# A hybrid decoder layer: one function table for Ln and Exp, a side projection in 16 products, another order list

## The chip, the cores and the metric

One Trainium2 chip, one core of it. The metric is the device time of one execution in microseconds (us), as the median of several runs. Five engines matter: PE (TensorE, matrix products), DVE (VectorE), ACT (ScalarE), POOL (GpSimd) and SP (SyncE, which issues most DMAs). Each engine works through its own queue in order.

## The reference

One decoder layer on x of 512 tokens by 1024 channels, in float32:

```python
x = x + 0.5 * swiglu(rms_norm(x, ffn1_norm), ...)            # d_ff = 2816
x = x + hybrid_mixer(rms_norm(x, mix_norm), ...)
x = x + 0.5 * swiglu(rms_norm(x, ffn2_norm), ...)
return rms_norm(x, final_norm)

def hybrid_mixer(h, ...):
    proj = h @ w_in                                          # one input projection
    gates = sigmoid(proj[..., aw + rs:] + gate_bias)
    y_attn = dilated_attention(proj[..., :aw], positions) @ attn_w_up
    y_rwkv = rwkv7_time_mix(token_shift(proj[..., aw:aw + rs], mu), ...)
    return (gates[..., :1024] * y_attn + gates[..., 1024:] * y_rwkv) @ w_o
```

`rwkv7_time_mix` has 16 heads of 64: a normalised key (`kk / sqrt(sum kk^2)`), a state recurrence over the tokens, a normalisation of its output per head (`(y - mean) / sqrt(var + eps)`), a bonus term and an output gate `sigmoid(zg) @ g2` with zg of 160 columns. `dilated_attention` has 3 groups of 4 heads, merged by their softmax denominators.

## The kernel before

Every large product is made of float32r products on PE. Weights and activations are split into a high and a low part (ACT copies the high part, DVE subtracts it), and a tile of 128 output channels by 512 tokens is the sum of 8 x 3 = 24 products of 128x128 by 128x512 (`mm3`: high x high, high x low, low x high). A weight tile of 512 KB comes by one DMA on SP's queue, three raw tiles ahead. The small products of the mixer are in plain float32.

The kernel has three parts: the first feed-forward, the mixer and the second feed-forward. In the mixer the main stream is a list of tiles, `MAIN`: two tiles of the small streams (`zwa`, `zg`), the 24 tiles of r, k and v (one of each per pair of heads), 16 gate tiles, 18 attention tiles (`aq`, `ak`, `av`, two halves by three groups), 8 tiles of `wout` (the recurrence's output projection, which needs all eight `yf`), two of `aup`, 8 of `wo`. Their order between `zwa`, `zg` and `wo` is written out by hand in `MAIN_ORDER`.

Between them runs side work, in three chains. `lora_all` and then `post(0)` to `post(7)` prepare one pair of heads each, from its k, r and v. `finish(0)` to `finish(3)` run the recurrence of two pairs each in 8 chunks one after another, and then `tail`, which normalises, gates and stores `yf`. `core(0)` and `core(1)` are the attention of one half each; `core` begins when its last key tile, `ak.<half>.2`, is there. A reciprocal square root (`rsqrt`) is an Ln and an Exp on ACT with one Newton step on DVE; `post` has one for the key and `tail` has one for the variance of each pair, 16 in all.

The mixer isn't issued as it is written. `Plan` records each instruction as a `Node` with a price (`note`), finds what depends on what, and simulates the five engines (`order`): it takes again and again the instruction that can start first, main products being placed between the side work. `emit` then issues the instructions in that order, which fixes every engine's queue. Prices are lines such as

```python
TABLES = {"Sigmoid": "sigmoid", "Tanh": "sigmoid", "Exp": "exp", "Ln": "exp", "Sqrt": "sqrt", "Silu": "silu"}
c = n / 2400 + 0.0136 if x.dtype == F32R else 4 * n / 2400 + 0.01      # us on PE; n is the free size
if nd.table and nd.table != table:                                     # ACT: another table
    c += 1.3
```

A plain float32 transpose of 128x128 is thus priced at 4 x 128 / 2400 + 0.01 = 0.223 us. The plan knows a switch of tables, and Ln and Exp are one table to it. The emitter issues no table load itself in the mixer; the tool chain places loads where an activation needs one.

`h_zg2` makes the last 32 columns of the gate stream: 24 products with 32 weight columns (`w_zg2`, split by `lora_w`), then `shift_evac` (token shift), a sigmoid and a split into `sg2`.

Of the kernel before, what the change touches and what calls it, by code (L numbers as in the profile page):

```python
# [45 lines left out]
WAHEAD = 2  # L46

MAIN_ORDER = """
k.0 r.0 v.0 k.1 r.1 v.1 gate.0 gate.1 gate.2 gate.3 k.2 gate.4 r.2 v.2 r.3 k.3 v.3 gate.5 gate.6 gate.7 gate.8 k.4 r.4
v.4 k.5 r.5 gate.9 v.5 gate.10 gate.11 gate.12 gate.13 gate.14 gate.15 k.6 r.6 v.6 k.7 r.7 v.7 aq.0.0 av.0.0 aq.0.1  # L50
ak.0.1 av.0.1 aq.0.2 ak.0.0 av.0.2 ak.0.2 av.1.2 av.1.0 aq.1.0 aq.1.1 ak.1.0 ak.1.1 av.1.1 aq.1.2 ak.1.2 wout.0 wout.1
wout.2 wout.3 wout.4 wout.5 wout.6 aup.0 wout.7 aup.1"""


PE, DVE, ACT, POOL, SP = "PE", "DVE", "ACT", "POOL", "SP"
LAT, SLACK, WINDOW, HOLD, SETTLE = 0.07, 0.2, 40, 0.0, 3.5
URGENT, SIDE, MAIN_MM = range(3)


class Node:  # L60
# [25 lines left out]
class Plan:  # L86


    TABLES = {"Sigmoid": "sigmoid", "Tanh": "sigmoid", "Exp": "exp", "Ln": "exp", "Sqrt": "sqrt", "Silu": "silu"}

    def __init__(self):
        self.on = False
# [38 lines left out]
    def note(self, eng, op, call, outs, ins, func=None):  # L131
        tags = [k[0] for k in map(self.slot, outs + ins) if k]
        if eng == PE:
            w, x = ins[0], ins[1]
            n, k, m = x.free_size(), w.shape[0], w.free_size()
            mode = (32 if k <= 32 else 64 if k <= 64 else 128, 32 if m <= 32 else 64 if m <= 64 else 128)
            c = n / 2400 + 0.0136 if x.dtype == F32R else 4 * n / 2400 + 0.01
            c = 0.018 if mode == (32, 32) else c * 0.5 if 64 in mode else c
            nd = self.open
            if nd is None:  # L140
                nd = self.open = Node(PE, self.cls, len(self.nodes))
                nd.mode = [mode, mode]
                self.placed(nd)
            elif nd.mode[1] != mode:
                c += 0.1
                nd.mode[1] = mode
            nd.cost += c
        else:
            self.open = None
            urgent = any(t.startswith(("wraw", "whi", "wlo")) for t in tags) or any(t.startswith("acc") for t in tags)  # L150
            nd = self.placed(Node(eng, URGENT if urgent else self.cls, len(self.nodes)))
            n = max([x.free_size() for x in outs + ins], default=0)
            psum = any(x.space == PSUM for x in outs + ins)
            if op == "dma_start":
                nd.cost = 0.43
                nd.lands = 4
                for c in outs[0].shape:
                    nd.lands *= c
            elif eng == ACT:
                nd.cost = 0.2 + n * 0.00084 if n else 1.3  # L160
                nd.table = self.TABLES.get(func)
            elif eng == POOL:
                nd.lock = op != "memset"
                nd.cost = 0.2 + n * (0.0022 if nd.lock else 0.00065)
            else:
                nd.lock = not psum
                nd.cost = 0.14 + n * {"reciprocal": 0.0063, "tensor_tensor_scan": 0.0028}.get(op, 0.00107)
        nd.calls.append(call)
        nd.writes += [(self.region(x), x.space == DRAM, self.slot(x)) for x in outs]
        nd.reads += [(self.region(x), x.space == DRAM, self.slot(x)) for x in ins]  # L170
# [46 lines left out]
    def order(self, keep):  # L217
# [19 lines left out]
        for nd in self.nodes:  # L237
            for tag in {k[0] for k in uses[nd]}:
                touch.setdefault(tag, []).append((nd, [k for k in nd.new if k[0] == tag], [k for k in uses[nd] if k[0] == tag and k in mortal]))

        def safe(nd):

            for tag in {k[0] for k in nd.new}:
                bufs = next(k[1] for k in nd.new if k[0] == tag)
                u = used.get(tag, 0) + sum(k[0] == tag for k in nd.new)
                if u > bufs:
                    return False
                rest = {}
                l = touch[tag] = [x for x in touch[tag] if x[0] not in done]
                for m, new, ends in l:  # L250
                    if m is not nd:
                        u += len(new)
                        if u > bufs:
                            return False
                    for k in ends:
                        n = rest[k] = rest.get(k, left[k]) - 1
                        if not n:
                            u -= 1
            return True

        while len(done) < len(self.nodes):
# [25 lines left out]
            if eng == SP or nd.lands:  # L287
                free[eng] = t + c
                dma = max(dma, t + c) + nd.lands / 190e3
                end = dma + 1.8  # L290
            elif eng == PE:
                if nd.mode[0] != mode:
                    c += 0.2 if nd.mode[0] == (128, 128) else 0.1
                mode = nd.mode[1]
                free[PE] = t + c
                end = t + c + 0.17
            else:
                if nd.table and nd.table != table:
                    c += 1.3
                    table = nd.table  # L300
                if nd.lock:
                    t = max(t, port)
                    port = t + c
                end = free[eng] = t + c
# [7 lines left out]
            for k in nd.new:  # L312
# [2 lines left out]
                freed[k[0]].remove(f)  # L315
                self.place[k[2]] = f[1]
            for k in uses[nd]:
                left[k] -= 1
                if not left[k] and k in mortal:
                    used[k[0]] -= 1  # L320
                    freed.setdefault(k[0], []).append((end, self.place.get(k[2])))
# [27 lines left out]
    def emit(self, tc, keep):  # L349
        self.on = False  # L350
        with tc.manual_schedule():
            for nd in self.order(keep):
                for tag, _, name in nd.new:
                    if tag in self.rings:
                        (pool, at), (shape, dt) = self.place[name], self.tiles[name]
                        self.homes[name] = pool.tile(list(shape), dt, tag=at, bufs=1, name=name)
                for f, args, kw in nd.calls:
                    f(*map(self.put, args), **{k: self.put(x) for k, x in kw.items()})  # L358
        self.nodes = []
# [332 lines left out]
def mixer(tc, a, env):  # L692
# [17 lines left out]
    with ExitStack() as st:  # L710
# [87 lines left out]
            split(z[:, 0:S], sg[:, 0, :], sg[:, 1, :])  # L798

        def h_zg2(ps):  # L800
            z = shift_evac(ps, 2, 32)
            A.activation(z[0:32, 0:S], z[0:32, 0:S], AF.Sigmoid)
            split(z[0:32, 0:S], sg2[0:32, :], sg2[32:64, :])
            A.copy(sg2[64:96, :], sg2[0:32, :].bitcast(F32))
# [318 lines left out]
        def tail(q, Qt, YT, raws):  # L1123
            for hl in range(2):
                hp = 2 * q + hl
                w = lora_w(raws[hl])
                A.copy(w[64:96, P:2 * P], w[64:96, 256 + P:512].bitcast(F32))
                sq = b2()
                A.activation(sq[:, 0:S], YT[:, hl, :], AF.Square)
                sh = split2(sq[:, 0:S])  # L1130
                ps = headsum(sh)
                rs = b2()
                V.tensor_scalar(rs[:, 0:S], ps, 1.0 / 64.0, GN_EPS, op0=ALU.mult, op1=ALU.add)
                rs = rsqrt(rs)
                V.scalar_tensor_tensor(rs[:, 0:S], YT[:, hl, :], col("ln_w", hp), rs[:, 0:S], op0=ALU.mult, op1=ALU.mult)
                bon = b2()
                Y.dma_start(bon[:, 0:S], bnd[:, hp, :])
                V.scalar_tensor_tensor(rs[:, 0:S], rs[:, 0:S], col("ln_b", hp), bon[:, 0:S], op0=ALU.add, op1=ALU.add)
                pg = mi()
                mm3(T, pg, (w[:, 0:P], w[:, 256:256 + P]), (sg[:, 0, :], sg[:, 1, :]), True, False)  # L1140
                T.matmul(pg, w[0:96, P:2 * P], sg2, start=False, stop=True)
                V.tensor_mul(rs[:, 0:S], rs[:, 0:S], pg)
                Y.dma_start(yf[:, hp, :], rs[:, 0:S])
# [123 lines left out]
        mrg = {}  # L1267
        ssq = acts.tile([P, S], F32, tag="ssqa", bufs=1, name="ssq_m")
        rstd = None
        wz = lora_w(lora_load(a["w_zg2"]))  # L1270
        for t in MAIN:
            n = t[0]
            w = wnext(t)
            if n in handlers:
# [8 lines left out]
                if n == "zg":  # L1283
                    ps = acc()
                    plan.stream = "main"
                    for k in range(DC):
                        plan.cls = MAIN_MM
                        mm3(T, ps[0:32, :], wsl((wz[:, 0:256], wz[:, 256:512]), k, 32), xk(k), k == 0, k == DC - 1)
                        plan.cls = SIDE
                        plan.cut()  # L1290
                    plan.stream = "main"
                    h_zg2(ps)
# [154 lines left out]
```

## Time and profile before

| | |
|---|---|
| time, median of 3 runs | 1404.8 us (1403.41 to 1405.29) |
| profiled execution, own time | 1407.91 us |
| its span, first to last instruction | 1406.1 us |
| PE, DVE, ACT, POOL busy | 97%, 59%, 43%, 1% of the span |
| granted PE clock, mean | 0.990 |
| mixer | some 365 to 1045 us of the span |

Products are pipelined, so that a busy PE isn't PE at its peak. "Idle before" an instruction is time in which its engine stood still, and the name behind it is what ended the wait. The granted clock is a share of 2.4 GHz. Lines of the profile are lines of the kernel file; in the mixer all instructions carry the emitter's line, L358, and are told apart by their tiles: `acc` is a main product, `mi` and `ch` are products of the side work, `b` is any work buffer, `wh` and `wl` are the split weights.

### The profile page before, as it was taken

What the parts mean: (1) busy time and instruction counts of PE and PEld (TensorE: products, weight loads), DVE (VectorE), ACT (ScalarE), POOL (GpSimd) and SP (SyncE); (2) the same over time, 40 slices, a digit from 0 to 9 for tenths busy, and PEclk for the clock granted to TensorE, in tenths of its full rate; (3) what the DMA queues carried; (4) which work ended last, traced back from release to release, by engine and by line L of the source; (5) the groups of instructions that cost most, each with busy time, mean ns of one, the idle gap of its engine ahead of it and who ended that gap; (6) DMA issues with size and microseconds to landing.
All of it is one profiled execution on the core that took longest, in us unless ns stands there. A gap on an engine that the chain in (4) does not pass through costs nothing. (4 is left out here: it accounts for less than half of the span.)

```text
span 1406.1 us, 21794 instructions
## 1 busy us (share of the span) xinstructions
PE 1363.9 (97%) x8852; PEld 1099.1 (78%) x8852; DVE 832.2 (59%) x1299; ACT 598.9 (43%) x918; POOL 19.9 (1%) x75
## 2 busy tenths in 40 slices
PE   7999999999999999999999999899999999999997
PEld 5888888888777876776876777677888888888886
DVE  6444444333578786876987887666654444443324
ACT  5232332222484454554655444686443232322222
POOL 0000000000000000000000000000000000000000
PEclk9999999999999999999999999999999999999998
DMA  5232323343564432423522412343652323233333
GB/s 191 93 103 93 103 90 101 96 129 109 161 208 134 145 94 82 126 84 102 148 82 60 122 52 64 127 153 111 195 179 90 101 95 101 94 92 93 99 100 109
DMA packets 83732, 158.53 MB, mean 113 GB/s; under 512 B 32368, under 2 KB 37232, under 8 KB 83632
## 3 DMA queue, kind: packets, MB, share of 16 engines
q1 hardware_dynamic: 82384, 154.78, 35.3%
q10 hardware_dynamic: 1152, 2.10, 0.4%
q8 instruction: 69, 1.13, 0.3%
q0 software_dynamic: 96, 0.26, 0.1%
q14 instruction: 31, 0.25, 0.1%
HBM read 135.88 MB, written 20.45 MB: 111 GB/s over the span
## 5 line engine op out<-in xcount | busy, mean ns | idle before, releaser
L377 ACT ACTIVATE wh<-wr 128x1024 fp32r<-128x1024 f32 (+1 forms) x140 | 144.0, 1029 | 468.4 <-PE facc L377 257.7
L377 PE MATMUL facc<-xhi,wh 128*128 128x512 f32 x704 | 276.0, 392 | 7.1 <-ACT wh L377 7.1
L377 PE MATMUL facc<-xlo,wh 128*128 128x512 f32 x704 | 274.7, 390 | 0.0
L377 PE MATMUL facc<-xhi,wl 128*128 128x512 f32 x704 | 274.5, 390 | 0.2 <-DVE wl L377 0.2
L377 DVE TENSOR_TENSOR wl<-wr,wh 128x1024 fp32r<-128x1024 f32 (+1 forms) x140 | 165.5, 1183 | 142.4 <-ACT wh L377 142.4
L358 PE MATMUL acc<-xhi,wh 128*128 128x512 f32 x544 | 227.1, 417 | 0.0
L358 PE MATMUL acc<-xlo,wh 128*128 128x512 f32 x544 | 215.1, 395 | 1.1 <-issue 1.1
L358 PE MATMUL acc<-xhi,wl 128*128 128x512 f32 x544 | 215.2, 396 | 1.0 <-DVE wl L358 1.0
L377 DVE TENSOR_TENSOR t<-facc,rstd 128x512 f32<-128x512 f32 x88 | 60.6, 691 | 223.0 <-PE facc L377 223.0
L377 PEld LDWEIGHTS facc<-xhi,wh 128*128 128x128 f32 x704 | 132.5, 188 | 36.2 <-ACT wh L377 7.5
L377 PEld LDWEIGHTS facc<-xlo,wh 128*128 128x128 f32 x704 | 132.5, 188 | 29.0 <-DVE xlo L377 0.9
L377 PEld LDWEIGHTS facc<-xhi,wl 128*128 128x128 f32 x704 | 132.5, 188 | 28.2 <-DVE wl L377 1.1
L377 PE MATMUL facc<-hhi,wl 128*128 128x512 f32 (+1 forms) x374 | 141.0, 377 | 0.7 <-DVE wl L377 0.7
L377 PE MATMUL facc<-hhi,wh 128*128 128x512 f32 (+1 forms) x374 | 141.0, 377 | 0.0
L377 PE MATMUL facc<-hlo,wh 128*128 128x512 f32 (+1 forms) x374 | 140.9, 377 | 0.0
L358 DVE TENSOR_TENSOR b<-b,b 128x512 f32<-128x512 f32 (+6 forms) x187 | 112.0, 622 | 21.9 <-ACT b L358 13.0
L358 ACT ACTIVATE wh<-wr 128x1024 fp32r<-128x1024 f32 x78 | 82.5, 1057 | 97.7 <-PE acc L358 71.1
L358 PEld LDWEIGHTS acc<-xhi,wh 128*128 128x128 f32 x544 | 103.5, 190 | 25.4 <-issue 0.6
L358 PEld LDWEIGHTS acc<-xhi,wl 128*128 128x128 f32 x544 | 103.3, 190 | 24.6 <-DVE wl L358 1.8
L358 PEld LDWEIGHTS acc<-xlo,wh 128*128 128x128 f32 x544 | 103.6, 190 | 19.5 <-issue 1.7
L358 ACT ACTIVATE b<-b 128x512 f32<-128x512 f32 (+4 forms) x155 | 92.1, 604 | 28.0 <-DVE b L358 16.4
L358 DVE TENSOR_TENSOR wl<-wr,wh 128x1024 fp32r<-128x1024 f32 x78 | 95.0, 1219 | 12.0 <-ACT wh L358 11.5
(125 smaller groups left out, 1476.8 us busy)
## 6 DMA issues: line engine op xcount, KB each, us to landing
wr<-in_ffn_gu_dram SPq DMA_DIRECT2D x87, 512.0 KB
wr<-in_w_in_dram SPq DMA_DIRECT2D x60, 512.0 KB
wr<-in_ffn_down_dram SPq DMA_DIRECT2D x34, 512.0 KB
wr<-in_ffn_down_dram SPq DMA_DIRECT2D x17, 384.0 KB
gdr<-b SPq DMA_DIRECT2D x16, 256.0 KB
wr<-in_w_out_dram SPq DMA_DIRECT2D x8, 512.0 KB
b<-gdr SPq DMA_DIRECT2D x16, 256.0 KB
wr<-in_w_o_dram SPq DMA_DIRECT2D x8, 512.0 KB
```

Source lines behind the costliest of these rows:

```text
L358: f(*map(self.put, args), **{k: self.put(x) for k, x in kw.items()})
L377: return f(*args, **kw)
```

## The change

The emitter keeps the table that it last loaded and issues a load by name whenever the next activation's table is another one; for Ln and Exp that is one set that holds both. The small projection multiplies a weight tile that holds the high and the low part side by side (and 8 columns more, so 72) with the high and the low activations: 16 products, whose two halves of 32 rows are added after. The variance in `tail` is scaled on ACT instead of DVE. `MAIN_ORDER` is another list of the same tiles. In the planner, prices of plain float32 products change, and so does that of a return to full products; `safe` remembers its answers, and they stay the same.

```diff
 MAIN_ORDER = """
-k.0 r.0 v.0 k.1 r.1 v.1 gate.0 gate.1 gate.2 gate.3 k.2 gate.4 r.2 v.2 r.3 k.3 v.3 gate.5 gate.6 gate.7 gate.8 k.4 r.4
-v.4 k.5 r.5 gate.9 v.5 gate.10 gate.11 gate.12 gate.13 gate.14 gate.15 k.6 r.6 v.6 k.7 r.7 v.7 aq.0.0 av.0.0 aq.0.1
-ak.0.1 av.0.1 aq.0.2 ak.0.0 av.0.2 ak.0.2 av.1.2 av.1.0 aq.1.0 aq.1.1 ak.1.0 ak.1.1 av.1.1 aq.1.2 ak.1.2 wout.0 wout.1
+gate.0 k.0 r.0 v.0 k.1 r.1 v.1 gate.1 gate.2 gate.3 k.2 r.2 v.2 gate.4 r.3 k.3 v.3 gate.5 gate.6 gate.7 gate.8 gate.9
+gate.10 k.4 r.4 v.4 k.5 r.5 gate.11 v.5 gate.12 gate.13 gate.14 gate.15 k.6 r.6 v.6 k.7 r.7 v.7 aq.0.1 aq.0.0 ak.0.0
+av.0.0 ak.0.1 av.0.1 aq.0.2 ak.0.2 av.0.2 av.1.0 aq.1.1 aq.1.0 av.1.1 ak.1.1 aq.1.2 ak.1.0 ak.1.2 av.1.2 wout.0 wout.1
 wout.2 wout.3 wout.4 wout.5 wout.6 aup.0 wout.7 aup.1"""
...
+def kw_pos(call):
+    return "tile_position" in call[2]
...
+    SETS = {"sigmoid": "sigmoid_and_others", "exp": "natural_log_exp_and_others", "sqrt": "sqrt_and_others"}
...
             c = n / 2400 + 0.0136 if x.dtype == F32R else 4 * n / 2400 + 0.01
-            c = 0.018 if mode == (32, 32) else c * 0.5 if 64 in mode else c
+            if x.dtype != F32R:
+                c = 0.118 if op == "transpose" else max(n, m) / 600 + 0.01
+            c = 0.033 if mode == (32, 32) and not kw_pos(call) else 0.018 if mode == (32, 32) else c * 0.5 if 64 in mode else c
...
                 if nd.mode[0] != mode:
-                    c += 0.2 if nd.mode[0] == (128, 128) else 0.1
+                    c += 0.27 if nd.mode[0] == (128, 128) else 0.1
...
         with tc.manual_schedule():
+            table = None
             for nd in self.order(keep):
+                if nd.table not in (None, table):
+                    table = nd.table
+                    tc.nc.scalar.preload_act_table_set(self.SETS[table])
...
         def h_zg2(ps):
-            z = shift_evac(ps, 2, 32)
+            t = b2()
+            A.copy(t[0:32, 0:S], ps[32:64, :])
+            V.tensor_add(t[0:32, 0:S], ps[0:32, :], t[0:32, 0:S])
+            z = shift_evac(t[:, 0:S], 2, 32)
...
                 rs = b2()
-                V.tensor_scalar(rs[:, 0:S], ps, 1.0 / 64.0, GN_EPS, op0=ALU.mult, op1=ALU.add)
+                A.activation(rs[:, 0:S], ps, AF.Identity, bias=eps[:, 1:2], scale=1.0 / 64.0)
                 rs = rsqrt(rs)
...
-        wz = lora_w(lora_load(a["w_zg2"]))
+        wzr, wz = lora_load(a["w_zg2"]), b2(F32R)
+        wz3 = wz[:, 0:512].rearrange("p (k s m) -> p k s m", s=2, m=32)
+        wzr3 = wzr[:, 0:256].rearrange("p (k m) -> p k m", m=32)
+        A.activation(wz3[:, :, 0, :], wzr3, AF.Copy)
+        V.tensor_sub(wz3[:, :, 1, :], wzr3, wz3[:, :, 0, :].bitcast(F32))
+        G.memset(wz[:, 512:520].bitcast(F32), 0.0)
...
-                        mm3(T, ps[0:32, :], wsl((wz[:, 0:256], wz[:, 256:512]), k, 32), xk(k), k == 0, k == DC - 1)
+                        for i, x_ in enumerate(xk(k)):
+                            T.matmul(ps[0:72, :], wz[:, 64 * k:64 * k + 72], x_, start=k + i == 0, stop=k + i == DC)
```

## Rows read from the trace of the kernel before

**Rows 1.** The page's first part: busy time and share of the span by engine.
```profile
PE 1363.9 (97%) x8852; PEld 1099.1 (78%) x8852; DVE 832.2 (59%) x1299; ACT 598.9 (43%) x918; POOL 19.9 (1%) x75
```
**Rows 2.** Stretches of the mixer: length, busy us of each engine (instructions), clock, DMA.
```profile
420.00:876.00 456.00, 441.12 (x4597) 341.18 (x4597) 365.78 (x691) 236.80 (x422) 15.00 (x49) 0.99 0.34 99
876.00:975.00 99.00, 88.41 (x541) 71.31 (x541) 61.08 (x112) 70.86 (x124) 0.00 (x0) 0.93 0.39 130
...
sum 680.00, PE 654.53 PEld 511.35 DVE 510.94 ACT 378.74 POOL 18.86; mean PE 163.63 PEld 127.84 DVE 127.73 ACT 94.68 POOL 4.72
...
925.00:960.00 35.00, 33.22 (x159) 27.32 (x155) 21.71 (x47) 32.20 (x59) 0.00 (x0) 0.95 0.43 143
```
**Rows 3.** Stretches again: one of four short slow ones, and the long one.
```profile
592.00:595.40 3.40, 3.40 (x10) 2.70 (x9) 3.16 (x6) 1.90 (x4) 0.00 (x0) 0.53 0.68 150
...
892.10:899.00 6.90, 5.62 (x31) 4.89 (x33) 5.52 (x7) 4.61 (x10) 0.00 (x0) 0.51 0.37 137
```
**Rows 4.** ACT's groups by form, 365 to 915 us, then 915 to 960 us.
```profile
L358 ACT ACT_TABLE_LOAD x35 | 44.9, 1283 | 2.6 <-DVE dc L358 1.4 <-DVE b L358 0.4
...
L358 ACT ACT_TABLE_LOAD x11 | 14.1, 1283 | 1.4 <-DMA b<-gdr 1.2
```
**Rows 5.** ACT in order of time in the last tail: start, us, instruction, idle before.
```profile
883.80 1.28 ACT L358 ACT_TABLE_LOAD   x1 [0.44 <-DVE b L358]
885.10 0.63 ACT L358 ACTIVATE b<-b 128x512 f32<-128x512 f32 x1
...
893.11 0.65 ACT L358 COPY b<-ch 128x512 f32<-128x512 f32 x1
```
**Rows 6.** PE in order of time, the same place.
```profile
893.38 1.97 PE L358 MATMUL ch<-cst,b 128*128 128x128 f32 x8 [5.47 <-ACT b L358]
```
**Rows 7.** PE in order of time near 530 us.
```profile
530.11 0.69 PE L358 MATMUL ch<-b,b 128*64 128x64 f32 x16 [1.49 <-DVE b L358]
```
**Rows 8.** ACT in order of time ahead of that gap.
```profile
523.82 1.28 ACT L358 ACT_TABLE_LOAD   x1
```
**Rows 9.** ACT in order of time at the mixer's start.
```profile
375.76 0.69 ACT L358 ACTIVATE rstd<-acc,eps 128x512 f32<-128x512 f32 x1 [2.97 <-PE acc L358]
```
**Rows 10.** PE in order of time: first product of the small projection, and the product behind it.
```profile
383.73 0.40 PE L358 MATMUL acc<-xhi,b 128*32 128x512 f32 x1
...
389.32 0.40 PE L358 MATMUL acc<-xhi,wh 128*128 128x512 f32 x1
```
**Rows 11.** ACT's groups by form, 365 to 915 us: a copy on 32 partitions.
```profile
L358 ACT COPY b<-ch 32x512 f32<-32x512 f32 x8 | 4.6, 579 | 5.9 <-PE ch L358 4.8 <-DVE b L358 1.0
```
**Rows 12.** Groups by form of DVE and ACT: operations on a PSUM tile.
```profile
L358 DVE TENSOR_SCALAR b<-mi 128x512 f32<-128x512 f32 x16 | 11.0, 684 | 1.7 <-PE mi L358 1.5
...
L358 ACT ACTIVATE b<-mi,vec 128x512 f32<-128x512 f32 x16 | 9.5, 667 | 1.1 <-PE mi L358 1.1
```
**Rows 13.** PE in order of time: two waits of the second attention half.
```profile
947.93 1.96 PE L358 MATMUL ch<-own,b 128*128 128x16 f32 x16 [1.78 <-ACT b L358]
...
970.81 1.52 PE L358 MATMUL acc<-b,wh 128*128 128x512 f32 x2 [2.03 <-ACT b L358]
```
**Rows 14.** PE's groups by form: transposes of the attention.
```profile
L358 PE MATMUL ch<-cst,b 128*128 128x128 f32 x60 | 9.4, 297 | 5.9 <-ACT b L358 5.9
```
**Rows 15.** What PE waited for from 365 to 1045 us: us, times, longest.
```profile
PE ch L358 <- ACT b L358: 8.8, 4, 5.5
PE ch L358 <- DVE b L358: 6.8, 8, 1.8
```
**Rows 16.** ACT in order of time: two neighbouring table loads of the first feed-forward.
```profile
23.41 1.28 ACT L377 ACT_TABLE_LOAD   x1
...
247.11 1.28 ACT L377 ACT_TABLE_LOAD   x1
```
**Rows 17.** PE's groups by form, 876 to 911 us: one of three kinds of main product.
```profile
L358 PE MATMUL acc<-xhi,wl 128*128 128x512 f32 x24 | 9.6, 402 | 0.0
```

More of the change, by code (lines that the diff above doesn't have):

```diff
@@ L239, in order, with find @@
                 touch.setdefault(tag, []).append((nd, [k for k in nd.new if k[0] == tag], [k for k in uses[nd] if k[0] == tag and k in mortal]))
+        known, moved = {}, dict.fromkeys(touch, 0)
         def safe(nd):
+            at = [moved[k[0]] for k in nd.new]
+            if known.get(nd, (0, 0))[0] != at:
+                known[nd] = at, find(nd)
+            return known[nd][1]
+        def find(nd):
             for tag in {k[0] for k in nd.new}:
@@ L317, in order @@
             for k in uses[nd]:
+                moved[k[0]] += 1
                 left[k] -= 1
```

## The prediction

> **What bounds the kernel now.** I read the page's first part, then the stages, then what PE waits for, then the instructions around the waits. The first part puts PE at 97% of the span and ACT at 43% [rows 1]. That average says little, so the second look is the table by stretches. Over the mixer (365 to 1045 us) PE is idle for 680.00 - 654.53 = 25.5 us; 456.00 - 441.12 = 14.9 of them lie from 420 to 876 us and 99.00 - 88.41 = 10.6 from 876 to 975, where the granted clock is 0.93; so nothing is left for the ends of the mixer [rows 2]. So the kernel is bound by PE everywhere, and a faster ACT or DVE is worth only what PE stands or runs slow for: the 25.5 us, plus the stretches at the lower clock. There are five of those in the mixer, each behind PE idle time: four of 3.4 us and one of 6.9 us [rows 3]. The granted clock there is 0.50 to 0.53, the 1.2 GHz level; half of what PE does in such a stretch is lost. The feed-forward parts run products back to back and nothing in the diff touches them.
>
> Why PE stands: its order is fixed by the planner's simulation. Where ACT or DVE is later than planned, PE blocks at the head of its queue although other products are ready. The planner's prices are in the code: it gives Ln and Exp one table ("exp"), so it plans no switch between them. The trace shows 35 table loads on ACT from 365 to 915 us, 1283 ns each [rows 4]: two before 390 us, one at 413 us, and 32 in 16 pairs, one in front of the Ln and one in front of the Exp of each of the 16 reciprocal roots (8 of `post`, 8 of `tail`). The planner knows of none of the 32.
>
> **The change part by part.** (1) *One table for Ln and Exp*: 32 loads x 1.283 us = 41 us leave ACT. On PE they are worth only the waits that they cause.
>
> The largest is the last `tail` (its two halves run two roots in a row). Four loads stand in the ACT queue from 883.80 us on, two to a root; the PSUM copy that PE needs comes out of that queue at 893.11 us [rows 5]. PE idles 5.47 us and then runs its next stretch at 0.51, with 5.62 us of work in it [rows 3, 6]. Four loads are 5.13 us, nearly the whole gap; without it PE doesn't stand long, and I let the slow clock go too: 5.13 + 5.62 / 2 = 7.9 us. The bounds are 0 (the copy waits for DVE instead) and 8.3.
>
> Three other gaps of PE end right behind such a pair, with a recurrence product late: 1.49 us at 530.11 [rows 7], its pair of loads from 523.82 us on [rows 8], and two like it, 1.07 us at 634 and 0.95 at 744. A pair gives back 2.57 us, more than each gap: 3.5 us, bounds 0 and 3.5.
>
> The Trainium skill (ScalarE: Activation LUTs, What ACT_TABLE_LOAD costs) prices a switch at about 2.66 us, a drain included. Rows show 1283 ns, and the next ACTIVATE right behind (883.80 + 1.28, then 885.10); by the page ACT would lose 85 us instead of 41, and four switches, 10.6 us, would take the whole gap with its slow clock: 8.3 us instead of 7.9, 17.3 in the sum below instead of 16.9. The row decides.
>
> (2) *The emitter's own loads.* The other switches stay, since sigmoid and exp remain two sets: 11 loads between 915 and 960 us [rows 4]. The emitter starts without a table, so it puts one load of the sqrt set ahead of `rstd`. It falls into 2.97 us that ACT idles there [rows 9]: 0, and 1.3 us if ACT had no gap.
>
> (3) *The small projection* goes from 24 products to 16. The 24 take 383.73 to 389.32 us, 0.233 each, and the 128-column product behind them takes as long as the first of them, 0.40 us from start to end [rows 10]. 8 x 0.233 = 1.9 us, and PE has no idle time there, so all of it counts. What is added: one ACT copy on 32 partitions, 0.58 us, one DVE add, near the 0.68 us of other 512-column operations [rows 11, 12], and a POOL memset. Their result `sg2` is first read by the first `tail`, behind the first `finish`; the ACT and DVE work hides behind main products that keep PE busy to 420 us (no idle there [rows 2]). Without that cover: 1.3 us.
>
> (4) *Variance scaled on ACT*: eight 684 ns operations leave DVE, eight of about 667 ns go to ACT [rows 12]. They lie in the same chain one after another, so the chain keeps its length: 0, bounds -0.7 and +0.7 (one operation in the last tail).
>
> (5) *The order list and the planner's prices.* Two moves can be named. `gate.0` goes to the front: k.0, r.0, v.0 and with them the first `post` come 24 products, 5.6 us, later; on SP a 512 KB weight load and a 256 KB store of the gate move with it, on DVE one evacuation. Main products fill PE meanwhile (no idle before 420 us): 0 there. The attention tiles change places among themselves; each aq or ak takes its weight load and four small shift copies on SP and a memset on POOL with it. In the last part av.1.2 now follows ak.1.2, so the score products of `core(1)` can begin one tile (5.6 us) earlier. PE waits for that chain twice: 1.78 us at 947.93 and 2.03 us at 970.81 [rows 13], with a 3.4 us slow stretch behind each: 3.8 + 3.4 = 7.2 us to be had. Against it, ACT is busy 32.20 of 35.00 us there [rows 2] and keeps its table switches. I take half, 3.6 us; bounds 0 and 7.2.
>
> The prices also change: a transpose from 0.223 us to 0.118; 60 of them keep PE busy for 9.4 us, 0.157 each [rows 14], so the new price is nearer. The rest of the gaps (25.5 - 5.5 - 3.5 - 3.8 = 12.7 us) and two slow stretches (3.4 us) depend on an order that no row shows. A plan nearer to the rows can remove up to 16.1 us; a different order can open as many gaps of the size of those seen. Value 0, bounds +10 and -16.
>
> *Sum*: 7.9 + 3.5 + 1.9 + 3.6 = 16.9 us. The profiled execution took 1407.9 us (span 1406.1 and 1.8 around it): 1391.0. The median of the runs is 3.1 us below the profiled one: 1388.
>
> **Rivals.** *The plan closes the rest too*: with loads and transposes priced as the rows have them, most of the 16.1 us and the other half of (5) go: 25 to 33 us, 1372 to 1380. For it: most gaps are under 2 us and end with DVE or ACT being late against the plan [rows 15]. Against: 6.8 us of it stand behind DVE, which the change hardly relieves.
>
> *The wait moves*: ACT no longer holds the last tail, but another queue does (DVE is the busiest helper from 420 to 876 us, 365.78 of 456.00 [rows 2]), and new gaps eat (5). Left are (3) and 5.1 us: 7 us, 1398.
>
> *The loads stay*: a pass of the tool chain places loads too, and might not count the emitter's. The Trainium skill (ScalarE activation tables: per-element evaluation and per-set limits, Table sets in the compiler and the runtime) says that the back end picks the greedy longest run per block, by which Ln and Exp would already share a set; the 16 pairs here say otherwise. As a mechanism of this kernel: if every Ln and Exp kept its load, only (3) and (5) are left, 5.5 us, 1399, or 1403 with (3) alone. Against it: the silu set, loaded by name once at 23.41 us, serves all 22 Silu of the first feed-forward without another load before 247.11 us [rows 16].
>
> *The filler runs out* (slower). From the last recurrence step (876 us) to the end of the input projections near 911 us, PE lives on some 70 main products, 24 of each of three kinds or one less [rows 17], 2.9 tiles; the output products need the last `yf`. The planner now thinks PE lighter by 148 transposes x 0.105 = 15.5 us and may spend those tiles earlier. Each missing tile is 5.6 us of idle PE. Without the stretch's own gain 16.9 - 7.9 = 9.0 us remain, so from the second missing tile on the kernel is slower; all three gone: 16.3 + 1.7 for the clock - 9.0 = +9, 1414. Against: both lists end with the same 18 attention tiles.
>
> **Chances.** A measurement can tell 0.2% (2.8 us) from no change. Forecast (12 to 22 us off) 0.56; the rest closes too 0.16; the wait moves 0.13; loads stay 0.04; filler runs out 0.08; no net change for other reasons 0.03. Faster: 0.56 + 0.16 + 0.13 and, of the loads' case, nothing much: 0.85. Slower 0.08, same 0.07. The forecast alone spans 1383 to 1393. For 8 in 10 the range must reach into the neighbours: down to 1374, where two thirds of the open 16.1 us and all of (5) are gone; up to 1401, above "the wait moves".
>
> **What would show it.** Table loads in the mixer fall from 46 to about 14, none inside a reciprocal root; the small projection has 16 products; PE idle behind ACT after the last recurrence falls from 5.9 us to under 1; no 6.9 us slow stretch; mixer idle near 13 us. I am wrong if PE's idle time falls and the time doesn't (mode switches grew), if idle behind DVE grows by as much, or if output products wait for `yf`.

## The result and the profile after

The changed kernel takes 1381.69 us (median of 4 runs, 1379.01 to 1382.79) against 1405.05 us (the kernel before, median of 4 runs now): a ratio of 0.9832, 95% interval 0.9814 to 0.985, 23.4 us less. The forecast was 1388, with 1374 to 1401 around it. The profiled span fell from 1406.1 to 1380.8 us.

The stretches of the mixer in the changed kernel, which answer to [rows 2], with a last row for one of its slow stretches:

```profile
420.00:876.00 456.00, 449.00 (x4706) 350.88 (x4705) 366.68 (x694) 215.30 (x419) 15.43 (x49) 0.99 0.35 102
876.00:975.00 99.00, 95.04 (x530) 75.73 (x529) 74.95 (x130) 69.02 (x122) 0.00 (x0) 0.98 0.44 148
...
sum 655.00, PE 643.77 PEld 506.46 DVE 505.61 ACT 341.52 POOL 19.36; mean PE 160.94 PEld 126.62 DVE 126.40 ACT 85.38 POOL 4.84
...
924.00:927.40 3.40, 3.40 (x11) 2.65 (x10) 2.34 (x10) 3.38 (x6) 0.00 (x0) 0.57 0.42 161
```

PE's idle time in the mixer is 655.00 - 643.77 = 11.2 us instead of 25.5: 7.0 instead of 14.9 up to 876 us, 4.0 instead of 10.6 behind it. Three slow stretches of 3.4 us are left where there were four and one of 6.9. What can be laid to rows is 25.5 - 11.2 = 14.2 us of idle, 4.6 us of half clock (half of what PE did in the slow stretches, 19.0 us before and 9.9 after) and 1.9 us of products: 21 of the 25 us that the span lost.

ACT's groups and its order of time in the last tail (answering to [rows 4, 5]), and PE's waits in the mixer (answering to [rows 15]):

```profile
L372 ACT ACT_TABLE_LOAD x12 | 15.4, 1283 | 0.2
...
L378 ACT ACTIVATE b<-mi,eps 128x512 f32<-128x512 f32 x8 | 5.4, 680 | 1.4 <-PE mi L378 1.3
...
874.38 0.67 ACT L378 ACTIVATE b<-mi,eps 128x512 f32<-128x512 f32 x1
875.08 1.96 ACT L378 ACTIVATE b<-b 128x512 f32<-128x512 f32 x3
876.95 0.57 ACT L378 COPY b<-ch 128x512 f32<-128x512 f32 x1
```
```profile
PE ch L378 <- issue: 4.1, 3, 2.2
PE ch L378 <- DVE b L378: 3.2, 5, 1.3
PE mi L378 <- DVE b L378: 2.0, 2, 1.8
PE ch L378 <- ACT b L378: 1.0, 1, 1.0
```

The emitter's line L372 issues 12 loads where 46 stood, three before 420 us and nine from 901 us on, so that none is left in a root; the variance, the Ln, the Exp and the square of a tail run on ACT without one between them, and the PSUM copy follows at once. PE waits 1.0 us for ACT in the whole mixer, at one place, instead of 11.1: the 8.8 of [rows 15], 2.0 ahead of an output product ([rows 13], the second) and 0.3.

### The profile page after: what moved, and what is told of

It is laid out like the page before. It is cut to its first block, busy times and chain, and to the rows that moved or that the text cites. A ratio compares the mean times of both kernels' runs of the same rounds, so it can differ in the third digit from the quotient of the medians.

```text
span 1380.8 us, 21768 instructions
## 1 busy us (share of the span) xinstructions
PE 1352.4 (98%) x8844; PEld 1094.7 (79%) x8844; DVE 826.6 (60%) x1292; ACT 561.3 (41%) x893; POOL 20.4 (1%) x76
## 4 chain that ended last, share of the span: by engine, by line
PE 91%; DVE 4%; ACT 2%; issue 1%; DMA 1%; SPq 0%; DVEq 0%; ACTq 0%; POOLq 0%
PE facc L397 52%; PE acc L378 28%; PE ch L378 6%; PE mi L378 5%; DVE b L378 3%; ACT b L378 1%; DVE wl L378 0%; ACT L372 0%; DVE X L397 0%; DMA b<-yf 0%; ACT wh L378 0%; PE acc L397 0%; DMA vec<-in_vec_dram 0%; SPq L378 0%; DVE xlo L378 0%
```

## The experiments

Every kernel is compared with runs of the kernel before on the same chip; those gave 1405 to 1407 us. "In the same order" means that the queue of each engine holds the same instructions in the same order but for those named.

**The loads alone.** The kernel before with the emitter's loads and nothing else; PE, DVE, SP and POOL keep their queues, ACT only loses loads.

```diff
             for nd in self.order(keep):
+                if nd.table not in (None, table):
+                    table = nd.table
+                    tc.nc.scalar.preload_act_table_set(self.SETS[table])
```

> The kernel before with the emitter's table loads alone; every engine's order stays that of the kernel before. Theory A (the 32 loads were what PE waited for): the two terms of the prediction for the loads, 7.9 + 3.5 = 11.4 us, come off: about 1394 us, PE idle in the mixer from 25.5 to about 16 us, the 5.5 us gap of PE at 893 us gone. Theory B (the order and the planner's prices did it): at most 5 us come off, 1400 us or more, and the gaps stay with other releasers.

Measured 1385.51 us (1384.99 to 1385.56), ratio 0.985 (0.9831 to 0.987): 21.2 us from the loads alone. The last tail in order of time on ACT, then on PE, with two stretches and PE's waits for DVE up to that tail:

```profile
864.22 0.28 ACT L363 ACTIVATE b<-ch 128x128 f32<-128x128 f32 x1 [1.57 <-PE ch L363]
...
868.43 3.81 ACT L363 ACTIVATE b<-b 128x512 f32<-128x512 f32 x6 [0.46 <-DVE b L363]
872.14 0.54 ACT L363 COPY b<-mi 128x128 f32<-128x128 f32 x2
872.46 0.65 ACT L363 COPY b<-ch 128x512 f32<-128x512 f32 x1
...
1022.81 0.69 ACT L382 ACTIVATE rstd<-acc,eps 128x512 f32<-128x512 f32 x1
```
```profile
872.73 1.09 PE L363 MATMUL ch<-cst,b 128*128 128x128 f32 x8 [0.23 <-ACT b L363]
...
420.00:864.10 444.10, 437.78 (x4640) 340.46 (x4639) 366.60 (x694) 201.51 (x395) 14.92 (x49) 1.00 0.34 104
876.00:975.00 99.00, 94.70 (x523) 77.08 (x520) 69.21 (x123) 65.83 (x115) 0.00 (x0) 0.97 0.41 140
...
PE ch L363 <- DVE b L363: 2.2, 4, 0.7
```

The gap of 5.47 us [rows 6] is 0.23 us. As the order is the same, the same instruction can be looked up in both traces. In the kernel before, two of these instructions, and the stretch that ends at the same product on PE (879.50 us there, 864.10 here), stand at

```profile
879.61 0.28 ACT L358 ACTIVATE b<-ch 128x128 f32<-128x128 f32 x1 [1.59 <-PE ch L358]
...
1044.85 0.69 ACT L377 ACTIVATE rstd<-acc,eps 128x512 f32<-128x512 f32 x1
...
420.00:879.50 459.50, 444.05 (x4643) 343.33 (x4641) 367.40 (x695) 237.61 (x425) 15.00 (x49) 0.99 0.34 100
```

The scaled copy at the end of the last recurrence starts 879.61 - 864.22 = 15.4 us earlier, the root of the second feed-forward 1044.85 - 1022.81 = 22.0 us earlier. So the last tail and what follows give 6.6 us, and 15 us had come before it. Over the same work from 420 us on, PE's idle time is 444.10 - 437.78 = 6.3 us instead of 459.50 - 444.05 = 15.4, and both slow stretches of that part are gone (clock 1.00). Most of the idle time that went had stood behind DVE: its waits by `ch` products fall from 6.8 us [rows 15] to 2.2, though DVE's queue is the same. One of the two slow stretches, at 714.6 us before, need not be the loads' doing: it stood behind a wait of 1.50 us with no releaser (the last section), which is 0.64 us here. Theory A holds in kind; its size, 11.4 us, was half of what came.

**All but the loads.** The changed kernel without those lines of the emitter.

```diff
-                if nd.table not in (None, table):
-                    table = nd.table
-                    tc.nc.scalar.preload_act_table_set(self.SETS[table])
```

> The changed kernel without the emitter's table loads, so that Ln and Exp switch again; its order is that of the changed kernel. Theory A: 11 us or more come back, 1393 us or above, because this order has been planned without the switches. Theory B: 5 us or less come back, about 1386 us.

Measured 1408.00 us (1405.33 to 1410.14), ratio 1.0013 (1.0001 to 1.0024). List, prices, projection and variance together gain nothing while Ln and Exp switch; with the loads they add 1385.5 - 1381.7 = 3.8 us by the medians, 2.5 us by the ratios, whose intervals overlap. 26.3 us came back, more than the loads gave alone; that this order has less room for them would explain it, but isn't shown.

**The old list, and the old prices, in the changed kernel.**

```diff
-gate.0 k.0 r.0 v.0 k.1 r.1 v.1 gate.1 gate.2 gate.3 k.2 r.2 v.2 gate.4 r.3 k.3 v.3 ...
+k.0 r.0 v.0 k.1 r.1 v.1 gate.0 gate.1 gate.2 gate.3 k.2 gate.4 r.2 v.2 r.3 k.3 v.3 ...
...
-                c = 0.118 if op == "transpose" else max(n, m) / 600 + 0.01
...
-                    c += 0.27 if nd.mode[0] == (128, 128) else 0.1
+                    c += 0.2 if nd.mode[0] == (128, 128) else 0.1
```

> The changed kernel with the old order list. Theory A: only the part of the order comes back, the 3.6 us of the prediction and some more, 1384 to 1388 us. Theory B: 8 us or more, 1390 us or above.

> The changed kernel with the planner's old prices for PE. Theory A: the prices matter little, 1382 to 1387 us. Theory B: the plan with old prices opens gaps again, 8 us or more, 1390 us or above.

Measured 1398.10 us (ratio 0.9941, 0.992 to 0.9962) and 1419.36 us (ratio 1.0092, 1.0072 to 1.0112). Either half of the new plan with the other half of the old is worse than both pairs: 1385.5 us old with old (with the old projection and variance too), 1381.7 us new with new. In the second, PE in order of time shows

```profile
938.29 0.80 PE L376 MATMUL acc<-xhi,wh 128*128 128x512 f32 x1 [10.08 <-ACT xhi L376]
```

which is the first output products waiting for the split of the last `yf`: what the rival of the filler that runs out describes, but with the new list and the old prices, not with the new prices to which the rival laid it. So the order is worth much more than theory A had, but as a matched pair; of list and prices alone neither is a gain.

**The last tail alone.** The table-only kernel with three loads put back into its last two roots (one set ahead of each Exp, the other ahead of the second Ln), in the same order.

```diff
+                if lns > 14 and func == "Exp" and lns < 17 and not self.after_exp:
+                    want = "exp_and_others"
```

> The table-only kernel with three loads put back, all in the two roots of the last tail, every engine's order as it was. Theory A as the prediction counted (this one place is the largest term: 5.13 us of loads and 2.8 us of slow clock for four): 3 x 1.283 + 2.8 = 6.6 us come back, 1392 us. Rival (the place was hidden, the gain lay in the many small gaps of the recurrence): under 2 us come back.

Measured 1388.58 us (1387.82 to 1390.16), ratio 0.9879 (0.9865 to 0.9892): 3.1 us by the medians, 4.6 by the spans (1388.4 and 1383.8). PE at that place, and the stretch:

```profile
875.76 1.97 PE L369 MATMUL ch<-cst,b 128*128 128x128 f32 x8 [4.22 <-ACT b L369]
...
877.96 0.63 PE L369 MATMUL acc<-xlo,wh 128*128 128x512 f32 x1
...
874.20:881.00 6.80, 5.24 (x27) 4.51 (x29) 5.57 (x8) 4.89 (x10) 0.00 (x0) 0.54 0.34 120
```

Three loads bring back a gap of 4.22 us and a slow stretch of 6.8 us, in which a main product takes 0.63 us; without them that place is at full clock. The wait grows by the loads that stand ahead of it: 0.23 us with none, 4.22 with three, 5.47 with four [rows 6], 1.3 us for each. So the mechanism of the largest term is as forecast. Its worth at the end is smaller than theory A's 6.6 us and larger than the rival's 2.

**Variance on DVE again**, in the places of the plan.

```diff
+                    if any(x is AF.Identity for x in args):
+                        tc.nc.vector.tensor_scalar(self.put(args[0]), self.put(args[1]), 1.0 / 64.0, GN_EPS, op0=ALU.mult, op1=ALU.add)
+                        continue
```

> The changed kernel with the variance scaled on DVE again, each of the eight operations in the place that the plan gave it, PE's order as it was. The prediction: no change within 0.7 us. Rival (DVE is the engine that PE waits for most, so its 5.5 us count): 2 us or more come back.

Measured 1382.16 us (1380.09 to 1383.66), ratio 0.9831 (0.9817 to 0.9844). Nothing, as predicted.

**Tanh gates**, first in the changed kernel, then in the table-only one; a sigmoid is half of one plus the tanh of half the argument, and tanh is in a set with exp. Behind the last Ln the emitter loads that set, `exp_and_others`, for Exp and Tanh.

```diff
-A.activation(gr[:, 0:S], gr[:, 0:S], AF.Sigmoid, bias=col("gate_bias", 8 + m))
-V.tensor_mul(gr[:, 0:S], ps, gr[:, 0:S])
+A.activation(gr[:, 0:S], gr[:, 0:S], AF.Tanh, bias=hgb[:, 8 + m:9 + m], scale=0.5)
+V.scalar_tensor_tensor(gr[:, 0:S], gr[:, 0:S], 1.0, ps, op0=ALU.add, op1=ALU.mult)
...
-V.tensor_add(x1[:, 0:S], ps, x1[:, 0:S])
+V.scalar_tensor_tensor(x1[:, 0:S], ps, 0.5, x1[:, 0:S], op0=ALU.mult, op1=ALU.add)
```

> The changed kernel with the output gates as tanh of half the argument, its factor of one half moved into the residual sum, so that the gates and the exponentials of the second attention half share a set: about eight loads go, 10 us of ACT between 900 and 930 us, with PE's order as it was. If the loads there hold PE as those in the roots did: the 1.0 us gap at 921 us and the 3.4 us slow stretch behind it go, 2.7 us, about 1379 us. If not (ACT is late only against itself there): within 0.5 us.

> The table-only kernel (old list, old prices, old small projection) with the output gates as tanh, as above, PE's order as it was. Its PE gaps of 1.8 us and 2.0 us in the second attention half, each with a 3.4 us slow stretch behind it, are those of the kernel before, which the prediction laid to the order. If the table switches between the gates and the exponentials make them: both go with their stretches, 5 to 7 us, 1379 to 1381 us. If the order makes them: under 1 us, 1385 us.

Measured 1380.22 us (ratio 0.9816, 0.9802 to 0.9829), which can't be told from the changed kernel, though in its trace the changed kernel's wait of 1.03 us at 921.54 us and the slow stretch behind it are gone; and 1381.14 us (ratio 0.983, 0.9818 to 0.9843) against 1385.51 of the table-only kernel, 4.4 us less by the medians, 2.8 by the ratios. The first line is the first wait of [rows 13] in the table-only kernel. The others are the second kernel's: its loads, the one in its last tail, PE behind that load, PE at the place of the first wait, and its last part.

```profile
925.55 1.62 PE L363 MATMUL ch<-own,b 128*128 128x16 f32 x13 [1.77 <-ACT b L363]
...
L360 ACT ACT_TABLE_LOAD x4 | 5.1, 1283 | 0.1
...
870.65 1.28 ACT L360 ACT_TABLE_LOAD   x1
...
873.73 1.09 PE L366 MATMUL ch<-cst,b 128*128 128x128 f32 x8 [1.50 <-ACT b L366]
...
923.71 1.85 PE L366 MATMUL ch<-own,b 128*128 128x16 f32 x16
...
876.00:975.00 99.00, 96.43 (x543) 79.19 (x544) 73.08 (x128) 54.29 (x108) 0.00 (x0) 1.00 0.47 154
```

With ten loads fewer, the first wait is gone and the clock is full; the second wait, 2.0 us, stays, without a slow stretch. So the switches between gates and exponentials made the first wait, in the old order too. One of the four loads left has its price: that of `exp_and_others` falls between the last Ln and its Exp, and the wait in the last tail is 1.50 us instead of 0.23.

**The small projection: more of it, and 16 products in the old order.** First 14 of its products issued twice and four times, by one and by three extra issues (the sum is then that of repeated products; three are shown); then, in the table-only kernel with tanh gates, 16 products in the places of the 24.

```diff
+                    for _ in range(3 if nd.eng == PE and args and args[0].shape[0] == 72 and not (kw["start"] or kw["stop"]) else 0):
+                        f(*map(self.put, args), **{k: self.put(x) for k, x in kw.items()})
```

> The changed kernel with 14 of the 16 products of the small projection issued twice (so its sum counts them twice), all else in the same order. If PE time at the mixer's start counts in full, as the prediction's 1.9 us for 8 products has it: 14 x 0.23 = 3.2 us more, about 1385 us. If later waits take it up: under 1 us.

> The changed kernel with 14 of the 16 products of the small projection issued four times (its sum counts them four times), all else in the same order: 42 x 0.23 = 9.7 us more of PE at the mixer's start. If such time counts in full: 1391 us. If later waits take up some 3 us, as doubling them suggested: about 1388 us. If they take up nearly all of it: under 1384 us.

> The changed kernel again, unaltered, for the comparisons of this call: 1381.7 us within 1.5.

> The table-only kernel with tanh gates, and the small projection in 16 products put into the places of the 24, so that every engine's order stays that of the kernel before. If PE's time there counts in full: 1.9 us below the same kernel with 24 products, about 1379 us, the fastest of all. If the new order is needed for it: 1381 us.

Twice: 1381.47 us (1379.98 to 1385.8); four times: 1396.01 us (1391.47 to 1398.15); the changed kernel again: 1380.63 us (1377.58 to 1384.2); 16 products in the old order: 1381.46 us (1379.66 to 1382.4), against 1381.14 with 24. By the medians 3.2 us more showed as nothing, 9.7 us more as 15, 1.9 us less as nothing.

The traces tell where it went. The first run of 32x32 products in the changed kernel and with 14 products twice; then, with tanh gates in the old order, the last of the 16 products, a wait behind them and the main product behind that wait, and last this main product in the kernel with 24:

```profile
496.54 1.29 PE L378 MATMUL ch<-b,b 32*32 32x32 f32 x128
...
499.67 1.29 PE L378 MATMUL ch<-b,b 32*32 32x32 f32 x128
...
387.00 0.40 PE L366 MATMUL acc<-xlo,b 128*72 128x512 f32 x1
...
392.24 2.13 PE L366 MATMUL mi<-b,b 128*128 128x512 f32 x7 [1.42 <-ACT b L366]
394.20 0.39 PE L366 MATMUL acc<-xhi,wh 128*128 128x512 f32 x1
...
393.55 0.40 PE L366 MATMUL acc<-xhi,wh 128*128 128x512 f32 x1
```

Twice: PE is 3.1 us later at 499.67 us, so up to there the added time counts in full. At the last such run it is 2.0 us earlier than the changed kernel (804.03 against 806.05), and what differs between them is waits with no releaser and a slow stretch (the last section), not waits for ACT (1.0 us in both) or DVE (5.8 and 5.6). Four times: 9.6 us later at that first run and 9.7 us in the profiled span (1390.5 against 1380.8); that execution, 1392.3 us, was one of the shortest of the six, and what the longer ones added is open. In the old order the 1.9 us is lost at once: the small projection ends 1.9 us earlier, but the main product behind the wait starts 0.65 us later. So in the new order the time counts until waits of its own size cover it, and in the old one it isn't gained at all.

## Why the prediction was right, and where its sizes were off

**What bounds the kernel** held: the time is PE's, and what changed is its idle time and its slow stretches. Loads fell from 46 to 12, none is left in a root, the long slow stretch is gone, and the mixer's idle time is 11.2 us where 13 was forecast. But the time is off the forecast's own span, 1383 to 1393, and lies in the range only because this had been widened towards the rival in which the rest closes too (1372 to 1380). Most of the waits did close as in that rival; the loads did it and not the plan.

**Term (1), 11.4 us, measured 21.2.** This is the mis-sized term. Its first part, the last tail, was 7.9 us, and 6.6 us came there and behind it. The second part was 3.5 us, counted from three gaps that end right behind a pair of loads; 15.4 us came from the part before. The count by neighbourhood was the fault, and with it the sentence that the change hardly relieves the 6.8 us behind DVE: with nothing but ACT's loads gone, 4.6 of them went. A wait that the trace puts down to DVE can thus be ACT's, passed on through DVE. Of the 15.4 us, idle time is 9.1 and the two slow stretches some 3.4, one of them perhaps not the loads'; some 3 us can't be laid to rows. The 32 loads held 41 us of ACT, and half of that came off the time.

**Term (2)**, the extra load of the sqrt set, was put at 0 and cost 0.3 us:

```profile
371.18 1.28 ACT L372 ACT_TABLE_LOAD   x1
372.47 0.72 ACT L397 ACTIVATE xhi<-X,vec 128x512 fp32r<-128x512 f32 x1
...
374.64 1.12 PE L378 MATMUL acc<-ssq,cst 128*128 128x512 f32 x2 [0.27 <-DVE ssq L397]
```

It stands ahead of the first feed-forward's last split, not in the gap of [rows 9], and PE waits 0.27 us for the sum of squares that follows from there. The table-only kernel has the same wait; the two kernels without the emitter's loads have none.

**Term (3), 1.9 us**: at its place it is right (24 products took 5.59 us; 16 take 387.48 - 383.80 = 3.7 us, 0.23 each). That it counts in full at the end isn't shown: in the new order added time counts in full up to 499.67 us and is covered later, in the old order nothing was left of it.

```profile
383.80 0.39 PE L378 MATMUL acc<-xhi,b 128*72 128x512 f32 x1
...
387.48 0.40 PE L378 MATMUL acc<-xhi,wh 128*128 128x512 f32 x1
```

**Term (4), 0**: right; the operation takes 680 ns on ACT, and back on DVE the time is the same.

**Term (5), 3.6 us, and the open rest, 0**: by the experiments the whole of list, prices, projection and variance is 3.8 us, given the loads, so the sum of (3) and (5), 5.5 us, was near. The reason was in part another: of the two waits in the second attention half, the first hung on the table switches beside it (1.0 us of it is left), and the second, 2.0 us with the loads alone, is gone in the changed kernel. That the open rest came out near 0 is luck as far as the rows go: either half of the plan with the other half of the old costs 16 to 38 us. The forecast undersized (1) by 10 us and oversized (3) and (5) by about 2. That makes 8 where 23.4 and 16.9 differ by 6.5: the loads alone were compared with runs of 1406.7 us, the changed kernel with 1405.05.

**Rivals.** The wait didn't move: PE's idle time behind DVE in the mixer fell from 9.6 to 5.8 us. The loads did go, so the tool chain counts the emitter's; in the trace before, the Trainium skill's greedy longest run (ScalarE activation tables: per-element evaluation and per-set limits, Table sets in the compiler and the runtime) wasn't to be seen, and the changed kernel without the emitter's loads has 44 again. What the filler's running out costs was seen with the old prices (10.08 us). The rival's reason for it was one-sided: beside the 148 transposes, which get 15.5 us cheaper, the diff raises 32 products of 128x16 from 0.037 to 0.223 us, 6.0 us, and some 120 returns to full products by 0.07, 8.7 us, so that the plan's PE time hardly changes.

## What to carry to other kernels

Where a planner fixes the queues, one price that it lacks can cost more than the waits right behind it: compare its switches, loads and prices with the trace before looking for a better order; here each order was good only with the prices that it had been found with. When a repeated small delay on a helper engine is removed, don't count only the gaps right behind it, nor only those that the trace puts down to that engine; bound it by all of the bound engine's idle time and slow clock in that part, and test it by removing it in an unchanged order. A version with tanh gates has 8 to 10 loads fewer and is worth trying where ACT is nearer to the bound; here 1380.2 us isn't told from 1380.6 to 1381.7.

## What the runs showed of the hardware that was not expected

PE waits with no releaser in the profile ("issue") stand inside or just behind long runs of 32x32 products, and they came and went between kernels with one order, and between two executions of one kernel: in the changed kernel 4.1 us in three of them, the longest with 126 of 128 products done, and in its second profile 5.8 us in four.

```profile
705.86 1.27 PE L378 MATMUL ch<-b,b 32*32 32x32 f32 x126
709.30 0.21 PE L378 MATMUL ch<-b,b 32*32 32x32 f32 x2 [2.17 <-issue]
```

What they wait for stays open; no run here was made for it. With a slow stretch they are large enough to hide a change of 3 us: at the second and the third run of 32x32 products the changed kernel waits 1.49 and 2.17 us, each with a slow stretch behind it; with the products issued twice it is 0.58 us and nothing, with no slow stretch there. So the medians of such small changes say little here.
